# Attention units in four parts, their matmul order fixed over three units with dense work in shares

## The chip, the cores and the metric

The program runs on one NeuronCore of a Trainium2 chip; nothing is split over cores. The metric is device time in microseconds from the start of an execution to its end. The kernel before took 1500.14 us (median of three executions, 1498.36 to 1502.25). TensorE does the matmuls and the transposes, VectorE (DVE in the profile), ScalarE (ACT) and GpSimd (POOL) the elementwise work, SyncE (SP) issues the DMAs.

## What is computed

One layer of a diffusion backbone for two groups of tokens with the same weights: 512 latent tokens and 128 context tokens, model width 1024, all in float32. The kernel keeps both groups side by side as T = 640 tokens, five tiles of 128.

```
u = norm(x) * (1 + scale) + shift;  u = u @ w_in           # one wide projection feeds four mixers
A  HGRN2 linear recurrence                                  # stage "hgrn"
B  windowed attention (+-128 tokens) with a sink logit      # 8 query heads, 2 key heads, head width 64
C  latent attention: q = norm(cq) @ w_uq, k, v = c_kv @ w_ukv, plus a rotary part of 32   # 8 heads
D  grouped attention, q and k normalised, rotary            # 8 query heads, 2 key heads
   B, C, D: p = softmax(q k^T * scale); o = p v             # latent queries see 128 cached context keys + latent keys
y = (sum over the four of (o_n @ w_branch[n]) * sigmoid(gates_n)) @ w_out
x = x + gate1 * norm(y);  x = x + gate2 * norm(relu(norm(x).. @ w_mlp_in)^2 @ w_mlp_out)
```

The outputs are the new activations of both groups and the context group's keys, values and states.

## The kernel before

**Dense matmuls.** A float32 operand is split into a high part in the fp32r format and a rest, and each product is three matmuls: high x high, high x rest, rest x high (`t_steps`, lines 365 to 367, with tokens as the moving side in two halves of 320; `tok_block`, lines 381 to 383, with 128 tokens as weights). One step of `t_steps` for a gate is 8 x 3 = 24 matmuls of 320 columns. Gates (`gate_steps`) are 16 such steps per branch, `merge` multiplies a branch's output by its `w_branch` and adds it to `yT`.

**An attention unit.** `unit` (line 800) is one pair of heads for one tile of 128 queries. With five key tiles (W = 640, all latent queries of D and C) each head has its scores in an own PSUM tile `sc` (two buffers of two banks), then a maximum (DVE, line 818), the exponential with its sum (ACT, line 819), a reciprocal (DVE, line 821) and the division (POOL, line 809). With fewer key tiles (B, and the context queries) both heads share one `sc`. Then the ten (or fewer) probability tiles are transposed, four to a PSUM tile `tp` (line 856), and each `tp` is copied out to `PT`, the first and third by ACT (line 858), the second by DVE (line 860). `tp` has two buffers, which the output `pv` (line 1009 or 1185) shares. The output products are 64 columns wide for each head (`pv`, two per key tile, each two instructions in the trace), and `o_evac` splits the result (ACT line 506, DVE line 142).

**The three attention stages.** B (`run_gqa(1, ...)`, line 1017) and D (`run_gqa(3, ...)`, line 1029) have 20 units each, C (`mla`) has 4 head pairs of 5 units. In B and D the second half of the queries is made between the tenth and eleventh unit, and the gates come behind all units. In C each head pair `jj` first makes its own operands: two steps from `cq` into an `sc` bank, split by `q_split` (ACT line 777, DVE line 779); transposes of the rotary queries into `pj` (line 1152, copied out at 1157 and 1158); for even `jj` six steps for values into `pj` (copied out at 1166); two steps for keys into an `sc` bank, copied out by `k_evac` (ACT 795, DVE and POOL by line 142 and 139). `pj` and `ada_ps` are one buffer each in a PSUM pool `psx` that takes the place of the two `mm` banks during C. The 27 steps of the later modulation (`side`, line 211, a load of 512 KB for each) are given out three after each unit of C.

**What sets the order.** The program is recorded by a framework that puts the instructions of each engine in an order of its own: it runs a timeline of its own over the recorded work and gives an engine the next instruction that is ready there. So the order before is not that of the code: gates and merges stand between units. `in_order(PE)` (line 73) makes the matmuls recorded inside it keep their recorded order among themselves; before, only the hgrn stage used it. Matmuls recorded outside may still stand between them.

## Time and profile before

| what | value |
|---|---|
| median of three executions | 1500.14 us |
| the profiled execution | 1502.2 us |
| its span, first to last instruction | 1500.4 us |
| granted TensorE clock, mean | 0.991 |
| TensorE matmul busy | 1430.5 us (95%) |
| DVE, ACT, POOL busy | 796.1, 481.4, 432.2 us |
| stage B, between merges and next keys | about 333 to 481 us |
| stage D | about 560 to 690 us |
| stage C, operands of the first head pair | about 795 to 812 us |
| stage C, units | about 812 to 940 us |

How to read it: a matmul's busy time overlaps the next one's, so the time from one matmul's start to the next one's is what it costs TensorE; an idle time in brackets behind a row is what TensorE stood still before it, with the instruction whose end let it go. The stretches are read off the timeline: B's units with the work between them, D's, and C's.

### The profile page before, as it was taken

The numbers are of one execution on the slowest core, as the hardware profiler recorded it, in microseconds if no ns is written. First come the engines' busy times: TensorE is split into PE (matmuls) and PEld (weight loads), VectorE is DVE, ScalarE is ACT, GpSimd is POOL, SyncE is SP. The second block draws the span as 40 slices with busy tenths as digits, with TensorE's granted clock in tenths as the row PEclk, the third lists the DMA queues.
The fourth block names the chain that finished last, engine by engine and source line by source line (L and its number), as shares of the span: only waits on it lengthen the run. The fifth ranks groups of instructions, "written<-read, shape, count | busy, mean of one in ns | idle before, by whom it ended". The sixth has DMA issues, their size and how long they took to land.

```text
span 1500.4 us, 26709 instructions
## 1 busy us (share of the span) xinstructions
PE 1430.5 (95%) x10969; PEld 1302.2 (87%) x10969; DVE 796.1 (53%) x1447; ACT 481.4 (32%) x1161; POOL 432.2 (29%) x456
## 2 busy tenths in 40 slices
PE   6999999899999999999998998998999999999996
PEld 5898998899898998999996677988898998898995
DVE  4347657476643788433725566746243444444446
ACT  4334333333443235442124565225220110110112
POOL 2015325243321545222213334124111111112114
PEclk9999999999999999999999999999999999999998
DMA  9421212121112131112224601221343223222221
GB/s 328 128 85 58 70 49 64 50 68 50 45 43 59 34 84 37 33 42 74 80 68 143 224 15 43 99 85 56 112 129 101 80 71 98 71 70 71 75 66 70
DMA packets 138225, 121.17 MB, mean 81 GB/s; under 512 B 22296, under 2 KB 119412, under 8 KB 138104
## 3 DMA queue, kind: packets, MB, share of 16 engines
q1 hardware_dynamic: 138104, 119.47, 26.4%
q8 instruction: 86, 1.41, 0.4%
q14 instruction: 35, 0.29, 0.1%
HBM read 115.96 MB, written 3.49 MB: 80 GB/s over the span
## 4 chain that ended last, share of the span: by engine, by line
PE 70%; issue 13%; DVE 8%; POOL 5%; ACT 2%; DMA 1%; POOLq 0%; DVEq 0%; SPq 0%; ACTq 0%
PE mm L365 12%; PE mm L366 11%; PE mm L367 11%; PE mm L381 4%; PE mm L382 4%; PE mm L383 4%; PE tp L856 3%; POOL wh L139 3%; PE pv L1009 3%; PE sc L383 3%; PE sc L381 2%; PE sc L382 2%; PE sc L949 2%; PE sc L950 2%; DVE wl L142 1%
## 5 line engine op out<-in xcount | busy, mean ns | idle before, releaser
L139 POOL TENSOR_SCALAR wh<-wr 128x1024 fp32r<-128x1024 f32 (+3 forms) x136 | 156.7, 1154 | 536.4 <-PE mm L366 290.4
L142 DVE TENSOR_TENSOR wl<-wr,wh 128x1024 fp32r<-128x1024 f32 (+3 forms) x160 | 198.9, 1247 | 160.0 <-POOL wh L139 120.8
L365 PE MATMUL mm<-hTh,wh 128*128 128x320 f32 x704 | 220.5, 313 | 2.0 <-DVE qA L520 0.9
L367 PE MATMUL mm<-hTh,wl 128*128 128x320 f32 x704 | 219.2, 311 | 0.0
L366 PE MATMUL mm<-hTl,wh 128*128 128x320 f32 x704 | 218.2, 310 | 0.0
L366 PE MATMUL mm<-h2Tl,wh 128*128 128x320 f32 x512 | 159.4, 311 | 1.1 <-DVE h2Tl L142 1.1
L365 PE MATMUL mm<-h2Th,wh 128*128 128x320 f32 x512 | 159.5, 312 | 0.0
L367 PE MATMUL mm<-h2Th,wl 128*128 128x320 f32 x512 | 159.2, 311 | 0.0
L809 POOL TENSOR_SCALAR P<-P,rden 128x640 f32<-128x640 f32 (+3 forms) x120 | 84.5, 713 | 184.0 <-DVE rden L821 80.7
L365 PEld LDWEIGHTS mm<-hTh,wh 128*128 128x128 f32 x704 | 132.2, 188 | 3.9 <-DVE qA L520 1.0
L367 PEld LDWEIGHTS mm<-hTh,wl 128*128 128x128 f32 x704 | 132.2, 188 | 0.9 <-issue 0.7
L366 PEld LDWEIGHTS mm<-hTl,wh 128*128 128x128 f32 x704 | 132.2, 188 | 0.5 <-issue 0.3
L382 PE MATMUL mm<-wl,hidh 128*128 128x512 f32 x320 | 124.8, 390 | 0.6 <-DVE wl L142 0.6
L381 PE MATMUL mm<-wh,hidh 128*128 128x512 f32 x320 | 125.3, 392 | 0.0
L383 PE MATMUL mm<-wh,hidl 128*128 128x512 f32 x320 | 124.6, 389 | 0.0
L1292 ACT ACTIVATE relu<-mm 128x320 f32<-128x320 f32 x64 | 28.0, 438 | 281.1 <-PE mm L367 281.1
L366 PEld LDWEIGHTS mm<-h2Tl,wh 128*128 128x128 f32 x512 | 97.1, 190 | 1.7 <-DVE h2Tl L142 1.5
L365 PEld LDWEIGHTS mm<-h2Th,wh 128*128 128x128 f32 x512 | 96.9, 189 | 0.7 <-issue 0.4
L367 PEld LDWEIGHTS mm<-h2Th,wl 128*128 128x128 f32 x512 | 97.0, 189 | 0.0
L1293 DVE TENSOR_TENSOR relu<-relu 128x320 f32<-128x320 f32 x64 | 40.4, 632 | 100.8 <-ACT relu L1292 100.8
L1305 DVE TENSOR_TENSOR y<-mm,y 128x512 f32<-128x512 f32 x70 | 48.2, 689 | 81.9 <-PE mm L383 81.9
L381 PE MATMUL sc<-wh,hTh 128*128 128x256 f32 (+2 forms) x224 | 72.0, 322 | 5.5 <-DVE tx L935 2.4
(355 smaller groups left out, 3238.4 us busy)
## 6 DMA issues: line engine op xcount, KB each, us to landing
wr<-in_w_in SPq DMA_DIRECT2D x56, 512.0 KB, 3.7
wada<-in_w_ada SPq DMA_DIRECT2D x48, 512.0 KB, 4.5
wr<-in_w_mlp_in SPq DMA_DIRECT2D x32, 512.0 KB, 4.0
wr<-in_w_mlp_out SPq DMA_DIRECT2D x32, 512.0 KB, 3.6
wr<-in_w_in SPq DMA_DIRECT2D x64, 64.0 KB, 2.1
wr<-in_w_branch SPq DMA_DIRECT2D x8, 512.0 KB, 4.1
wr<-in_w_branch SPq DMA_DIRECT2D x16, 256.0 KB, 4.1
wr<-in_w_out SPq DMA_DIRECT2D x8, 512.0 KB, 3.6
```

The source lines that it names most:

```text
L139: G.tensor_scalar(out=out, in0=src, scalar1=1.0, scalar2=1.0, op0=ALU.mult, op1=ALU.mult)
L142: V.tensor_tensor(out=out, in0=src, in1=f(hi), op=ALU.subtract)
L365: PE.matmul(out=ps[:, 0:tn], lhsT=wh, rhs=a, start=(k == 0), stop=False)
L366: PE.matmul(out=ps[:, 0:tn], lhsT=wh, rhs=b, start=False, stop=False)
L367: PE.matmul(out=ps[:, 0:tn], lhsT=wl, rhs=a, start=False, stop=(k == nk - 1))
L381: PE.matmul(out=ps[:, 0:n], lhsT=a, rhs=w[k][0], start=(start and k == 0), stop=False)
L382: PE.matmul(out=ps[:, 0:n], lhsT=a, rhs=w[k][1], start=False, stop=False)
L383: PE.matmul(out=ps[:, 0:n], lhsT=b, rhs=w[k][0], start=False, stop=(stop and k == nk - 1))
L809: G.tensor_scalar(out=Pt[:, i, 0:W], in0=Pt[:, i, 0:W], scalar1=rden[:, i:i + 1], scalar2=1.0, op0=ALU.mult, op1=ALU.mult)
L856: PE.transpose(out=tp[:, kk, i], in_=Pt[:, i, 128 * (kt + kk):128 * (kt + kk) + 128], identity=ident)
L1009: PE.matmul(out=out, lhsT=Vt[:, ks[kt], 64 * a:64 * a + 64], rhs=PTa, start=start, stop=stop)
L1305: V.tensor_tensor(out=ys, in0=ps, in1=ys, op=ALU.add)
```

## The change

`unit` no longer emits a whole unit: it returns four parts, the scores of the first head (or of both, where they share a tile), the scores of the second, the transposes, and the output products. `run_units` emits them under `in_order(PE)` as a pipeline over three units: first scores of the new unit, products of the oldest, a share of dense work, second scores of the new unit, a share, transposes of the middle unit, a share. `Fill` gives out the dense work: in B and D the second queries (`query_steps`, 0.9 each) and the branch's 16 gate steps (1.0 each), 0.33 a share; in C the operands of the next head pair (`heads`, 0.25 a step and a share), now all through the one `pj` buffer, also the two `cq` steps and the two key steps that used `sc` banks. The first head pair's operands are made ahead of all units. The modulation steps are given out two after each unit's products, not three after each unit.

```diff
+    class Fill:
+        def __init__(self, steps):
+            self.steps, self.due = steps, 0.0
+        def give(self, share):
+            self.due += share
+            while self.due > 0:
+                self.due -= next(self.steps, 1e9)
+        def rest(self):
+            for _ in self.steps:
+                pass
...
-        if W > 512:
...
+        def wide(i):
+            sv = sc_tile()[:, :, 0:W // 2]
+            for a in range(2):
+                score(sv[:, a], i, a * (W // 2), W // 2)
+            V.tensor_reduce(out=negm[:, i:i + 1], in_=sv, axis=AX.XY, op=ALU.max, negate=True)
+            S.activation(out=Pt[:, i, 0:W].rearrange("p (a n) -> p a n", a=2), in_=sv, func=AF.Exp,
+                         bias=negm[:, i:i + 1], accum_out=den[:, i:i + 1])
+            V.reciprocal(out=rden[:, i:i + 1], in_=den[:, i:i + 1])
+            weigh(i)
+        def both():
...
         PT = at.tile([128, 5, 2, 128], F32, tag="PT", name="PT")
-        for j, kt in enumerate(range(0, nk, 2)):
-            kn = min(2, nk - kt)
-            tp = tp_tile().rearrange("p (k i) t -> p k i t", i=2)
-            for i in range(2):
-                for kk in range(kn):
-                    PE.transpose(out=tp[:, kk, i], in_=Pt[:, i, 128 * (kt + kk):128 * (kt + kk) + 128], identity=ident)
-            if j % 2 == 0:
-                S.activation(out=PT[:, kt:kt + kn], in_=tp[:, 0:kn], func=AF.Copy)
-            else:
-                V.tensor_copy(out=PT[:, kt:kt + kn], in_=tp[:, 0:kn])
-        o = pv_tile()
-        for kt in range(nk):
-            for a in range(2):
-                pv_mm(o[64 * a:64 * a + 64, 0:128], a, kt, PT[:, kt, a], kt == 0, kt == nk - 1)
-        o_evac(n, c, 128 * qt, o[:, 0:128])
+        def turn():
+            for j, kt in enumerate(range(0, nk, 2)):
+                kn = min(2, nk - kt)
+                tp = tp_tile().rearrange("p (k i) t -> p k i t", i=2)
+                for i in range(2):
+                    for kk in range(kn):
+                        PE.transpose(out=tp[:, kk, i], in_=Pt[:, i, 128 * (kt + kk):128 * (kt + kk) + 128], identity=ident)
+                if j % 2 == 0:
+                    S.activation(out=PT[:, kt:kt + kn], in_=tp[:, 0:kn], func=AF.Copy)
+                else:
+                    V.tensor_copy(out=PT[:, kt:kt + kn], in_=tp[:, 0:kn])
+        def products():
+            o = pv_tile()
+            for kt in range(nk):
+                for a in range(2):
+                    pv_mm(o[64 * a:64 * a + 64, 0:128], a, kt, PT[:, kt, a], kt == 0, kt == nk - 1)
+            o_evac(n, c, 128 * qt, o[:, 0:128])
+        if W > 512:
+            return lambda: wide(0), lambda: wide(1), turn, products
+        return both, lambda: None, turn, products
+    def run_units(units, beside, after=lambda: None):
+        cur = old = None
+        units = iter(units)
+        with in_order(PE):
+            while True:
+                new = next(units, None)
+                if new is None and cur is None and old is None:
+                    break
+                if new:
+                    new[0]()
+                if old:
+                    old[3]()
+                    after()
+                beside()
+                if new:
+                    new[1]()
+                beside()
+                if cur:
+                    cur[2]()
+                beside()
+                old, cur = cur, new
...
-        def queries(j2):
+        def query_steps(j2, Q):
             QQ = big(F32R, 2, 2, T, name="Q")
-            Q = [QQ[:, a] for a in range(2)]
+            Q += [QQ[:, a] for a in range(2)]
             wq = wgroup(q_cols(OFF[qn], j2), 0, 256)
...
                 q_split(tp[:, 0:2], [x[:, :, 128 * tt:128 * tt + 128] for x in Q], 0.125)
+                yield 0.9
+        def queries(j2):
+            Q = []
+            for _ in query_steps(j2, Q):
+                pass
             return Q
-        return queries, K, Vt
+        return queries, query_steps, K, Vt
...
-    def run_gqa(n, queries, Q0, K, Vt, tiles, sink, bands):
-        for j2 in range(2):
-            Q = queries(j2) if j2 else Q0
-            for qt, i in [(qt, i) for qt in range(5) for i in range(2)]:
-                ks, j = tiles(qt), 2 * j2 + i
...
+    def run_gqa(n, query_steps, Q0, K, Vt, tiles, sink, bands):
+        Q1, sig = [], [big(F32, 4, T, name="sig") for _ in range(2)]
+        second = query_steps(1, Q1)
+        def dense():
+            yield from second
+            yield from gate_steps(n, sig)
+        def units():
+            for j2 in range(2):
+                for qt, i in [(qt, i) for qt in range(5) for i in range(2)]:
+                    if j2:
+                        for _ in second:
+                            pass
+                    yield one(Q1 if j2 else Q0, j2, qt, i)
+        def one(Q, j2, qt, i):
+            ks, j = tiles(qt), 2 * j2 + i
...
+        fill = Fill(dense())
+        run_units(units(), lambda: fill.give(0.33))
+        fill.rest()
+        return sig
...
-    run_gqa(1, queries, Q0, K, Vt, swa_tiles, True, swa_bands)
-    sig = gates(1)
+    sig = run_gqa(1, query_steps, Q0, K, Vt, swa_tiles, True, swa_bands)
...
-        for jj in range(4):
+        def heads(jj, got):
             QQ = big(F32R, 4, T, name="mQ")
             Qa, QR = [QQ[:, a] for a in range(2)], [QQ[:, 2 + a] for a in range(2)]
             def ev(ps, t0, tn):
                 q_split(ps, [Qa[a][:, t0:t0 + tn] for a in range(2)], MS)
-            t_block(wu['uq'][0], 128 * jj, cX, ev, bank=sc_bank)
+            for _ in t_steps(wu['uq'][0], 128 * jj, cX, ev, bank=pj_tile):
+                yield 0.25
             for t4, tts in ((0, range(4)), (4, range(4, 5))):
                 tp = pj_tile().rearrange("p (i t) -> p i t", t=128)
                 n4 = len(tts)
                     V.scalar_tensor_tensor(out=to[32:64], in0=src, scalar=MS, in1=f(to[0:32]), op0=ALU.mult,
                                            op1=ALU.subtract)
                     copy_r(to[64:128], f(to[0:64]))
+                yield 0.25
             if jj % 2 == 0:
                 wv = [(x[0][:, 128 * jj:128 * jj + 256], x[1][:, 128 * jj:128 * jj + 256]) for x in wu['ukv'][1]]
                 for kt in range(6):
                     ps = tok_block(wv, 256, kX, kt, pj_tile())
                     for i in range(2):
                         S.activation(out=Vs[jj + i][:, kt], in_=ps[:, 128 * i:128 * i + 128], func=AF.Copy)
-            Vt = Vs[jj]
+                    yield 0.25
             K = new_K("mK")
             def ev(ps, t0, tn):
                 for a, b in ((t0, min(t0 + tn, T)), (max(t0, T), t0 + tn)):
                     if a < b:
                         k_evac(ps[:, a - t0:b - t0], K, a, b - a)
-            t_block(wu['ukv'][0], 128 * jj, kX, ev, halves=((0, 384), (384, 384)), bank=sc_bank)
-            for qt in range(5):
-                ks = full_tiles(qt)
-                def score(out, a, k0, kn):
-                    t = slice(128 * qt, 128 * qt + 128)
-                    b = slice(ks[0] * 128 + k0, ks[0] * 128 + k0 + kn)
-                    qk_mm(out, Qa[a][:, t], K_part(K, b.start, kn), a, last=False)
-                    PE.matmul(out=out, lhsT=QR[a][:, t], rhs=KRo[:, b], start=False, stop=True)
-                def pv_mm(out, a, kt, PTa, start, stop):
-                    PE.matmul(out=out, lhsT=Vt[:, ks[kt], 64 * a:64 * a + 64], rhs=PTa, start=start, stop=stop)
-                unit(n, jj, (0, 1), qt, len(ks), score, pv_mm)
-                side_steps(3)
+            for _ in t_steps(wu['ukv'][0], 128 * jj, kX, ev, halves=((0, 384), (384, 384)), bank=pj_tile):
+                yield 0.25
+            got += [Qa, QR, K]
+        got = [[] for _ in range(4)]
+        preludes = [heads(jj, got[jj]) for jj in range(4)]
+        for _ in preludes[0]:
+            pass
+        fill = Fill(iter(()))
+        def units():
+            for jj in range(4):
+                fill.rest()
+                fill.steps, fill.due = (preludes[jj + 1] if jj < 3 else iter(())), 0.0
+                for qt in range(5):
+                    yield one(jj, qt, *got[jj])
+        def one(jj, qt, Qa, QR, K):
+            ks, Vt = full_tiles(qt), Vs[jj]
...
+        run_units(units(), lambda: fill.give(0.25), lambda: side_steps(2))
```

The order on TensorE, at three places. In the names, `sc` is a PSUM tile of scores, `tp` of transposed probabilities `P`, `pv` of output products, `mm`, `mp` and `pj` of projections and small transposes; `hT`, `cq` and `ckv` are the normalised tokens and the latent query and key inputs, `w` weights, `ident` the identity of a transpose. Where a name has a number, each number is one use of a buffer.

TensorE in stage B before, around the products of one unit:

```order
L856 MATMUL tp<-ident,P 128x128 x4
L1009 MATMUL pv<-PT,Vt 64x128 x4
L382 MATMUL mm<-wl,hTh 128x256
L383 MATMUL mm<-wh,hTl 128x256
L919 MATMUL mp<-ident,txr 128x128 x2
L1009 MATMUL pv<-PT,Vt 64x128 x4
L856 MATMUL tp<-ident,P 128x128 x4
```

and in the changed kernel, in the same stage, around the products of one unit:

```order
L993 MATMUL sc<-K,Q 128x128
L994 MATMUL sc<-K,Q 128x128
L993 MATMUL sc<-K,Q 128x256
L994 MATMUL sc<-K,Q 128x256
L1067 MATMUL pv<-PT,Vt 64x128 x8
L365 MATMUL mm<-hTh,wh 128x320
L366 MATMUL mm<-hTl,wh 128x320
```

The products of a unit stood in two halves with other work between; now all of them stand in one piece, between the newest unit's scores and a share of dense work, and the eight transposes of the unit between stand together ahead of those scores. Counted over stage B, the runs of `pv` go from 35 to 20, in D from 21 to 20, in C from 25 to 21, and those of `ada_ps` in C from 18 to 13.

TensorE in stage D before, between two units:

```order
L856 MATMUL tp_6331<-ident_82,P_6299 128x128 x2
L919 MATMUL mp_6751<-ident_82,txr_6720 128x128 x2
L1009 MATMUL pv_6335<-PT_6318,Vt_5399 64x128 x10
L856 MATMUL tp_6371<-ident_82,P_6351 128x128 x4
L949 MATMUL sc_6456<-K_5397,Q_5663 128x320
L950 MATMUL sc_6456<-K_5397,Q_5663 128x320
```

and in the changed kernel:

```order
L367 MATMUL mm_6663<-hTh_138,wl_6660 128x320
L865 MATMUL tp_6689<-ident_82,P_6555 128x128 x4
L865 MATMUL tp_6695<-ident_82,P_6555 128x128 x4
L865 MATMUL tp_6701<-ident_82,P_6555 128x128 x2
L993 MATMUL sc_6710<-K_5397,Q_5663 128x320
L994 MATMUL sc_6710<-K_5397,Q_5663 128x320
```

Before, only the first of a unit's three `tp` tiles stood ahead of eight score matmuls and the other two behind them; now the three follow each other with nothing between, in each of the 16 units with five key tiles in D and the 16 in C.

TensorE at the start of stage C before:

```order
L365 MATMUL sc_9100<-ckv_7858,wh_8930 128x384
L366 MATMUL sc_9100<-ckv_7858,wh_8930 128x384
L367 MATMUL sc_9100<-ckv_7858,wl_8931 128x384
L1152 MATMUL pj_9033<-ident_82,qv_8938 64x128 x3
L211 MATMUL ada_ps_9008<-wada_9172,cpad_120 32x256 x4
L211 MATMUL ada_ps_9008<-wada_9178,cpad_120 32x256 x4
L211 MATMUL ada_ps_9008<-wada_9184,cpad_120 32x256 x4
L1152 MATMUL pj_9033<-ident_82,qv_8938 64x128
L949 MATMUL sc_9120<-mK_9088,mQ_9010 128x320
L950 MATMUL sc_9120<-mK_9088,mQ_9010 128x320
```

and in the changed kernel:

```order
L367 MATMUL pj_9022<-cq_7857,wl_8923 128x320
L1214 MATMUL pj_9033<-ident_82,qv_8938 64x128 x4
L1214 MATMUL pj_9044<-ident_82,qrp_8939 64x128
L381 MATMUL pj_9052<-wh_8930,ckv_7858 128x256
L382 MATMUL pj_9052<-wl_8931,ckv_7858 128x256
L383 MATMUL pj_9052<-wh_8930,ckv_7858 128x256
L381 MATMUL pj_9058<-wh_8930,ckv_7858 128x256
```

The operands of the first head pair used `sc` banks and `pj`, with modulation steps and scores between, and the values came behind the first scores; now twelve groups, two of `cq`, two of transposes, six of values, two of keys, follow each other in `pj`, and the first scores stand behind all of them.

## Rows read from the trace of the kernel before

**Rows 1.** The page, busy time and share of the span by engine:

```profile
PE 1430.5 (95%) x10969; PEld 1302.2 (87%) x10969; DVE 796.1 (53%) x1447; ACT 481.4 (32%) x1161; POOL 432.2 (29%) x456
```

**Rows 2.** Busy time by stretch: length, then PE, PEld, DVE, ACT, POOL, clock, DMA:

```profile
333.00:481.00 148.00, 147.14 (x1135) 133.74 (x1134) 80.14 (x191) 61.92 (x173) 42.72 (x58) 1.00 0.19 49
560.00:690.00 130.00, 127.06 (x1068) 119.00 (x1063) 65.47 (x141) 61.64 (x152) 42.09 (x52) 1.00 0.14 39
795.10:811.60 16.50, 12.47 (x94) 9.25 (x93) 11.72 (x26) 9.53 (x19) 9.38 (x14) 0.95 0.40 133
811.60:939.80 128.20, 116.74 (x1023) 90.72 (x1021) 77.54 (x168) 74.41 (x206) 50.12 (x75) 0.98 0.32 103
```

**Rows 3.** Waits of TensorE, in D and in C's units: total us, times, longest:

```profile
PE pv L1009 <- ACT PT L858: 1.6, 3, 0.7
...
PE pv L1185 <- ACT PT L858: 3.4, 5, 1.2
```

**Rows 4.** Timeline, TensorE in B: start, busy us, instruction, idle before:

```profile
390.96 0.44 PE L1009 MATMUL pv<-PT,Vt 128*64 128x128 f32 x4
391.32 0.66 PE L856 MATMUL tp<-ident,P 128*128 128x128 f32 x4
392.73 0.44 PE L856 MATMUL tp<-ident,P 128*128 128x128 f32 x2 [0.75 <-ACT PT L858]
...
449.23 0.31 PE L366 MATMUL mm<-hTl,wh 128*128 128x320 f32 x1
449.47 0.66 PE L1009 MATMUL pv<-PT,Vt 128*64 128x128 f32 x8
450.06 0.66 PE L856 MATMUL tp<-ident,P 128*128 128x128 f32 x4
```

**Rows 5.** Timeline, transposes of a unit of C and the copies behind them:

```profile
866.58 1.03 PE L856 MATMUL tp<-ident,P 128*128 128x128 f32 x8
867.21 0.60 ACT L858 ACTIVATE PT<-tp 128x512 f32<-128x512 f32 x1 [0.87 <-PE tp L856]
867.86 0.44 PE L856 MATMUL tp<-ident,P 128*128 128x128 f32 x2
```

**Rows 6.** Timeline of C: first matmul of a projection and its copy:

```profile
801.85 0.39 PE L365 MATMUL sc<-ckv,wh 128*128 128x384 f32 x1
802.62 0.98 ACT L795 ACTIVATE mK<-sc 64x384 fp32r<-64x384 f32 x2 [1.36 <-PE sc L367]
...
810.38 0.63 PE L1182 MATMUL sc<-ckv,mQ 128*128 128x320 f32 x1 [0.58 <-POOL mQ L139]
...
865.34 0.28 PE L381 MATMUL pj<-wh,ckv 128*128 128x256 f32 x1
865.90 0.28 ACT L1166 ACTIVATE mVt<-pj 128x128 f32<-128x128 f32 x1 [0.77 <-PE pj L383]
...
871.45 0.36 PE L365 MATMUL sc<-cq,wh 128*128 128x320 f32 x1
872.38 0.60 PE L1152 MATMUL pj<-ident,qv 128*64 128x128 f32 x4
872.58 0.88 ACT L777 ACTIVATE mQ<-sc 64x320 fp32r<-64x320 f32 x2 [0.89 <-PE sc L367]
```

**Rows 7.** Instructions of C by line and shape: count, busy us, mean ns, idle:

```profile
L819 ACT ACTIVATE P<-sc,negm 128x640 f32<-128x640 f32 x32 | 25.3, 794 | 14.9 <-DVE negm L818 13.0 <-DVE rden L821 1.4 <-POOL mQ L139 0.5
L819 ACT ACTIVATION_READ_ACCUMULATOR P<-sc,negm 128x1 f32 x32 | 6.4, 200 | 0.0
L1157 ACT ACTIVATE mQ<-pj 32x512 fp32r<-32x512 f32 x8 | 4.7, 585 | 3.1 <-DVE mQ L1158 2.3 <-PE pj L1152 0.6
...
L818 DVE TENSOR_REDUCE negm<-sc 128x1 f32<-128x640 f32 x32 | 26.4, 824 | 15.5 <-PE sc L1182 15.0
L779 DVE SCALAR_TENSOR_TENSOR mQ<-sc,mQ 64x320 fp32r<-64x320 f32 x16 | 7.8, 488 | 5.4 <-ACT mQ L777 5.2
L1158 DVE SCALAR_TENSOR_TENSOR mQ<-pj,mQ 32x512 fp32r<-32x512 f32 x8 | 5.5, 682 | 1.5 <-ACT mQ L1157 1.3
L142 DVE TENSOR_TENSOR mK<-sc,mK 64x384 fp32r<-64x384 f32 x8 | 4.4, 555 | 0.4 <-ACT mK L795 0.2
...
L809 POOL TENSOR_SCALAR P<-P,rden 128x640 f32<-128x640 f32 x32 | 25.5, 800 | 43.1 <-DVE rden L821 36.1 <-PE pj L383 6.8
L139 POOL TENSOR_SCALAR mK<-mK 64x768 fp32r<-64x768 f32 x8 | 7.5, 934 | 7.6 <-DVE mK L142 7.2
```

67 lines of the change are left out of this document (29 added, 38 removed).

## The prediction

> **What bounds the kernel now.** The page first: TensorE is busy 1430.5 us of the 1500.4 us span, no other engine above 53% [rows 1]. So the time is TensorE's matmuls plus what it stands still, and no matmul is added or taken away by the change: only its order moves, and with it the idle time and the small costs of going from one kind of matmul to another. How much there is to win stands in the view by stretches [rows 2]. In B TensorE is busy 147.14 of 148.00 us, so 0.86 is idle; in D 127.06 of 130.00, idle 2.94; where C makes its first head pair's operands 12.47 of 16.50, idle 4.03; in C's units 116.74 of 128.20, idle 11.46. All four together are 19.3 us, 1.3% of the time. The list of waits says what the largest single items are: the output products wait for ACT's copies of the transposed probabilities, 1.6 us in D and 3.4 in C's units [rows 3]. The timelines then give the price of a step [rows 4 to 6], the groups by line the durations of the other engines' parts [rows 7].
>
> The sum is made against the profiled execution, 1502.2 us (span 1500.4 and 1.8 around it), which is 2.1 above the median of 1500.14.
>
> **Stage B.** The rows before have products in two runs of four, 390.96 to 391.32, so 0.36 us a run, and in one run of eight, 449.47 to 450.06, so 0.59 [rows 4]. Two runs of four cost 2 x 0.36 - 0.59 = 0.13 more. A run also costs its entry: the dense matmul ahead of it takes 449.23 to 449.47, 0.24, where six dense matmuls in a row take 871.45 to 872.38, 0.155 each [rows 6], so 0.09. Together 0.22 for a run that goes, and B loses 15 of its 35: -3.3. Of the 0.86 idle I take 0.7 away, because a whole step of dense work now stands between a unit's transposes and its products, which covers the 0.75 wait for a copy that the rows show once [rows 4]. B: -4.0; bounds -4.2 and 0 (if a run's entry depends on its neighbours and not on its being one more).
>
> Gates that come behind all units in the code now come among them; in the order before they already stood among units, so nothing is gained by that again. VectorE, ACT and POOL have the same work.
>
> **Stage D.** The same argument takes away the 2.94 idle; one product run less is nothing. But the three `tp` tiles of a unit with five key tiles now follow each other, `tp` has two buffers, and the third tile needs the first one's copy. The one place in the rows that has this order shows the price: transposes start at 866.58, ACT's copy starts at 867.21 and takes 0.60, the third tile's transposes start at 867.86, so 1.28 behind the first [rows 5]. Eight transposes by themselves take some 0.8 to 0.9 (the eight are busy 1.03, the two 0.44, so 0.1 for each further one). The wait is 0.4 to 0.5; I take 0.42. What is queued behind it on TensorE is the next unit's scores and the oldest unit's products, so nothing fills it. 16 units: +6.7. D: -2.9 + 6.7 = +3.8. Bounds for a unit: 0, if the split order before lost as much in changes of kind, and 0.75, the longest wait for such a copy in these rows.
>
> **Start of C.** Twelve groups through the one buffer `pj`, with nothing between: each must be copied out before the next one's first matmul. The chain by rows:
> two halves of the queries, each 1.13 from first matmul to ACT's copy (871.45 to 872.58), 0.44 for one of its two ACT instructions and two VectorE instructions of 0.488 [rows 6, 7]: 2 x 2.55 = 5.1;
> four rotary transposes 0.60, ACT 0.585, VectorE two of 0.682 [rows 6, 7]: 2.6, and the fifth by itself 1.2 (my estimate, a quarter of the columns, the fixed part stays);
> six value groups, 0.56 to the copy (865.34 to 865.90) and two copies of 0.28 [rows 6]: 6.7;
> the first key half 0.77 (801.85 to 802.62), 0.49 for ACT, two VectorE instructions of 0.555 [rows 6, 7]: 2.4; the second half until its last part has gone through VectorE and POOL (0.934, [rows 7]) and is multiplied: 3.0.
> Together 21.0 us. It begins where the key projection stood, less the twelve query matmuls that were done earlier: 801.85 - 12 x 0.155 = 800.0. First scores are then complete at 821.0. Before, their last part starts at 810.38 [rows 6] and they are complete at about 811.3. The step costs +9.7. The values' 18 matmuls are then done (a credit of some 2.2) and the modulation steps that filled the stretch before are not (a debit of about the same). C's start: +10. Bounds: +7 (the queue of copies split better between ACT and VectorE) and +12.
>
> The Trainium skill, "Perfetto Trace Analysis", section "Matmuls", speaks against this step: independent matmul groups should rotate through different PSUM banks, so that the copying out of one overlaps the next one's matmuls. The trace agrees so far as it goes: where the key halves used `sc` banks, ACT's copy of one ran beside the other's matmuls. By the rule alone, the loss would be the copies' part of the chain above, some 14 of the 21, and the sum 4 higher.
>
> **Units of C.** What goes: the 11.5 idle, all of it, because dense groups stand between a unit's parts; four product runs (25 to 21) and five modulation runs (18 to 13) by 0.22 each: -2.0. What comes: twelve units more with the three `tp` tiles in a row (four had it already), 12 x 0.42 = +5.0. And the next head pairs' groups go through the one `pj` as well, one a share. For the second head pair I walk through it, from the start of the first scores, with the durations above, each queue in order and ACT's exponential (0.794 and 0.200, [rows 7]) ahead of the copy that follows it, as the changed program has it:
> scores 0 to 0.9, VectorE's maximum (0.824) to 1.85, exponential to 2.95; the first query group is multiplied 0.9 to 1.9, but ACT's copy of it starts at 2.95 and VectorE is done at 4.4. The second scores end at 2.8, and the second query group waits for `pj` from there: 1.6. Its copy waits in the same way for the second exponential and VectorE is done at 7.8; it was multiplied by 5.4, so the rotary group waits 2.4. The fifth transpose waits 2.0 behind VectorE, where the next unit's maximum stands between the two halves of the rotary copy; the first key group 1.2; and a `tp` tile 1.2, because ACT has the key copy ahead of it.
> Together 8.4. The third and fourth head pairs have a unit's products and modulation steps between some of the groups; the same walk gives about 7 and 6. (The value groups' open part of 0.6 is covered.) That is 21. The lower bound is without exponentials in the way: only what a copy takes longer than the scores or transposes (0.9, 1.28) that stand between two shares: 3.7 in the second head pair, 1.2 in each of the others, 6 in all. I take 18, near the walk, since its order is that of the queues, with a little off because single steps may be shorter in a row. While TensorE waits there, the middle unit's transposes and the newest unit's scores are queued behind. Sum for the units: -11.5 - 2.0 + 5.0 + 18 = +9.5.
>
> Other queues: the 27 loads of 512 KB for the modulation go out two a unit instead of three, and the DMA share in this stretch is 0.32 [rows 2], so they come in time. On POOL the keys' copies (0.934) can stand ahead of a division (0.800); the transposes of that unit come a unit later (scores 0.9 twice, transposes 1.28, products and modulation steps some 1.8: 4.9 at least), and a head's chain of maximum, exponential and division is 0.82 + 0.99 + 0.80 = 2.6, so I cost it at nothing; without the cover it is 0.9 for each of six.
>
> **Sum.** -4.0 + 3.8 + 10 + 9.5 = +19.3. 1502.2 + 19.3 = 1521.5 for an execution like the profiled one, 1519 for the median.
>
> **Rivals.**
> *The clock falls* (slower still). The start of C had a granted clock of 0.95 with TensorE busy 12.47 of 16.50 us, where B and D had 1.00 with next to no idle [rows 2]. In the new chain TensorE has some 6.6 us of matmuls in 21. If the clock goes to the 1.2 GHz level there, each of them takes twice as long, and they are all in the chain: +6.6, and some 2.4 in the first unit behind it, +9 in all: 1528. Against it: 0.95 is still near full.
> A sentence apart: the Trainium skill, "TensorE: Matmul & The Clock Gate", Part 1, has the clock follow TensorE's activity, which is what would make this rival happen.
> *Covered after all* (no change). The projections' waits in C's units vanish, because the scheduler's order on ACT and VectorE puts the copies ahead and scores, products and modulation steps cover them: -4.0 + 3.8 + 10 - 11.5 - 2.0 + 5.0 = +1.3: 1503.5, less 2.1, so 1501.
> *All covered* (faster). The third tile also costs no more than the split order did: -4.0 - 2.9 + 10 - 11.5 - 2.0 = -10.4, so 1490. It rests on one mechanism, whether ACT's copy of the first `tp` tile is out by the time the eighth transpose is done; it decides against me if ACT's copies start less than 0.25 behind a tile's first transpose. For it: each part now lies a whole part behind what it needs, and the softmax chain of 2.6 is shorter than a unit. Against it: [rows 5] shows the copy's start at 0.63. That the order isn't what the change says is no rival here: the rows of the order show it.
>
> **How the numbers follow.** Forecast 0.62, by itself 1504 to 1530 (C's start 7 to 12, the waits in C's units 6 to 21, D's tiles 0 to 12, B -4.2 to 0). Clock 0.16, no change 0.11, faster 0.11. The range 1499 to 1533 holds the forecast, the clock and the case without change, and leaves the faster one out. A measurement of this kernel tells about 0.3% from no change, so from 1495.6 to 1504.6: faster 0.11, same 0.11, slower 0.78.
>
> **What would show it.** In the changed profile: B's stretch shorter by 3 to 4 us with hardly an idle row; in D about 16 waits of `tp` for ACT's copy, 0.4 each; ahead of C's first scores about 20 us in which TensorE is busy a third, with `pj` waiting for VectorE and ACT; in C's units `pj` waits of some 18 us, and products that no longer wait for ACT. The prediction is wrong if the first scores of C stand within 5 us of where they stood, or if `pj` hardly waits inside the units, or if the time is won in D and B beyond 7 us, which no row here would explain.

## The result: 5% slower, where 1.3% was forecast

The changed kernel takes 1574.41 us (median of four, 1572.3 to 1580.63) against 1500.08 (median of four; the 1500.14 above is that of three): a ratio of 1.0502, 95% interval 1.0469 to 1.0534. Forecast were 1519 and a range to 1533. The direction was right, the size was not: 74 us where 19 stood in the sum. (Of y3_gates_behind below, one execution, the profiled one, ran at a mean clock of 0.2 and took 6678 us; it stands in no time here.)

The page of the changed kernel, its busy time and its clock line (40 slices of the span; 9 is nine tenths or more), and under it the clock line of the kernel before:

```profile
PE 1447.7 (92%) x10969; PEld 1318.1 (84%) x10969; DVE 795.6 (51%) x1447; ACT 483.8 (31%) x1161; POOL 432.3 (28%) x456
...
PEclk9999999999999999999996799999999999999999
...
PEclk9999999999999999999999999999999999999998
```

Against [rows 1] the matmuls are the same 10969, VectorE, ACT and POOL work as long as before, and TensorE is busy 17 us longer for the same work. That fits the clock: in the stages below 51 us of its busy time fall at the 1.2 GHz level and not 10, and half of the difference, some 21 us, would be the loss if matmuls take twice as long there (an estimate from these numbers). The other 53 us of the 70 that the span grew are TensorE standing still.

Where they went is read by cutting both traces at equal points: the same matmul, with the same matmuls done by then (the first scores of B, the first scores of D, the first matmul on `cq`, 73 matmuls later, the end of C's units). Lengths in us, from the timelines:

| kernel | median us | ratio, interval | B | D | C, first operands | C, units |
|---|---|---|---|---|---|---|
| before | 1500.1 | | 200.8 | 268.2 | 10.7 | 136.2 |
| changed | 1574.4 | 1.0502 (1.0469 to 1.0534) | 206.3 | 296.0 | 34.0 | 150.6 |

Behind these points both kernels need 558 us, the same to a few tenths. (The prediction's own C start ended with complete scores, 3 to 5 us later, so C is best read as one: 146.9 against 184.6.)

Busy time by stretch: length, then PE, PEld, DVE, ACT, POOL, clock, DMA, for B, D and C's two parts, in the kernel before and then in the changed one:

```profile
326.10:526.90 200.80, 195.25 (x1488) 180.38 (x1487) 117.33 (x290) 75.92 (x207) 64.96 (x85) 0.99 0.21 51
526.90:795.10 268.20, 264.64 (x2006) 255.05 (x2006) 140.47 (x298) 89.67 (x234) 80.17 (x96) 1.00 0.22 60
795.10:806.40 11.30, 9.50 (x78) 7.36 (x76) 9.31 (x21) 7.82 (x15) 5.34 (x7) 1.00 0.16 49
806.40:942.10 135.70, 122.01 (x1056) 94.71 (x1055) 80.74 (x177) 76.87 (x212) 54.17 (x82) 0.97 0.34 109
...
325.10:531.40 206.30, 193.19 (x1489) 181.99 (x1488) 114.20 (x288) 74.24 (x207) 67.58 (x86) 0.98 0.21 49
531.40:827.40 296.00, 274.81 (x2007) 260.92 (x2006) 143.43 (x300) 92.77 (x234) 77.78 (x96) 0.98 0.21 54
827.40:860.80 33.40, 16.23 (x72) 12.31 (x72) 11.87 (x24) 11.57 (x29) 8.14 (x12) 0.68 0.05 16
860.80:1011.90 151.10, 124.36 (x1059) 98.48 (x1060) 78.46 (x173) 73.90 (x198) 51.91 (x77) 0.90 0.30 98
```

What the reader is to see: D stood idle for 3.6 us and C's first operands for 1.8, and now it is 21 and 17; and the granted clock of C's first operands is 0.68, a mean of the 1.2 and the 2.4 GHz level. The busiest of the other engines, VectorE, is busy for 36% to 55% of these stretches. So no other engine is full, and yet TensorE waits.

For whom it waits in the first 70 us of D: total us, times, longest:

```profile
PE mp L957 <- DVE rden L826: 5.5, 1, 5.5
PE mm L365 <- DVE sig L1024: 3.5, 1, 3.5
PE mp L957 <- DVE ms L196: 2.0, 1, 2.0
PE tp L865 <- ACT PT L867: 1.6, 2, 0.9
PE mm L381 <- DVE tx L979: 1.3, 1, 1.3
PE mp L957 <- DVE txr L775: 1.1, 1, 1.1
```

The output products' wait of [rows 3] isn't in this list, as the change wanted (behind 600 us, D still has one of 1.9). What stands there now is `mp` (the transposes of a second query step) and the merge, and both wait for VectorE. The longest one, in the timeline of that place (TensorE, VectorE and POOL; start, busy us, instruction, idle before):

```profile
585.85 2.06 POOL L139 TENSOR_SCALAR wh<-wr 128x1024 fp32r<-128x1024 f32 x2
...
586.40 0.39 ACT L974 ACTIVATE tx<-mm 128x256 f32<-128x256 f32 x1 [2.40 <-PE mm L383]
...
586.93 2.05 DVE L142 TENSOR_TENSOR wl<-wr,wh 128x1024 fp32r<-128x1024 f32 x1 [1.95 <-POOL wh L139]
...
588.88 0.31 PE L994 MATMUL sc<-K,Q 128*128 128x320 f32 x1
588.90 0.40 DVE L976 TENSOR_REDUCE ssq<-tx 128x4 f32<-128x256 f32 x1
...
592.10 0.16 DVE L196 TENSOR_SCALAR ms<-ssq 128x4 f32<-128x4 f32 x1
...
593.40 0.42 DVE L979 TENSOR_TENSOR tx<-mm,rs 128x256 f32<-128x256 f32 x1
593.86 0.70 DVE L981 TENSOR_TENSOR tx<-tx,qg_b 128x256 f32<-128x256 f32 x1
594.48 0.15 DVE L826 RECIPROCAL rden<-den 128x1 f32<-128x1 f32 x1
594.71 0.66 PE L957 MATMUL mp<-ident,tx 128*128 128x128 f32 x2 [5.51 <-DVE rden L826]
```

Read it from below. The transposes at 594.71 need the normalised queries, a chain of ACT, VectorE, POOL and VectorE again behind the projection that ended at 586.4. VectorE could have begun at 586.8, but next in its queue is the split of a gate's weights (`wl`). It had been waiting 1.95 us for POOL's half, starts at 586.93 and takes 2.05; so the sum of squares starts at 588.90. A maximum, a split of queries and another weight split, rows that are left out here, stand in the chain's way after that: its next link (`ms`) starts only at 592.10. TensorE has its next scores, transposes and gates behind these two small transposes and may do none of them. (The list names `rden`, the last VectorE instruction that ended before; what was needed is `tx` ahead of it.) Before, the framework was free to put other work there.

In C's units the list is that of the one buffer:

```profile
PE pj L1214 <- DVE mQ L784: 6.9, 3, 2.4
PE tp L865 <- ACT PT L867: 4.2, 11, 0.8
PE pj L365 <- DVE mQ L784: 3.3, 3, 1.2
PE pj L365 <- DVE mQ L1220: 2.6, 2, 1.3
PE mm L365 <- DVE rden L826: 1.8, 1, 1.8
PE pj L1214 <- DVE mQ L1220: 1.7, 1, 1.7
PE pj L381 <- DVE mQ L1220: 1.3, 1, 1.3
```

The `pj` rows shown are 15.8 us, 17.0 with one shorter row.

### The profile page after: what moved, and what is told of

Same layout as the page of the kernel before. It is cut to its first block, busy times and chain, and to the rows that moved or that the text cites. A ratio compares the mean times of both kernels' runs of the same rounds, so it can differ in the third digit from the quotient of the medians.

```text
span 1570.5 us, 26738 instructions
## 1 busy us (share of the span) xinstructions
PE 1447.7 (92%) x10969; PEld 1318.1 (84%) x10969; DVE 795.6 (51%) x1447; ACT 483.8 (31%) x1161; POOL 432.3 (28%) x456
## 4 chain that ended last, share of the span: by engine, by line
PE 65%; issue 13%; DVE 9%; ACT 5%; POOL 5%; DMA 1%; SPq 0%; POOLq 0%; DVEq 0%; ACTq 0%
PE mm L365 11%; PE mm L366 11%; PE mm L367 11%; PE mm L381 4%; PE mm L382 3%; PE mm L383 3%; POOL wh L139 3%; PE sc L383 2%; PE sc L381 2%; PE sc L382 2%; PE tp L865 2%; PE pv L1067 2%; PE sc L993 2%; PE sc L994 1%; DVE wl L142 1%
## 5 line engine op out<-in xcount | busy, mean ns | idle before, releaser
L865 PE MATMUL tp<-ident,P 128*128 128x128 f32 x456 | 71.4, 286 | 14.7 <-ACT PT L867 11.6
```

The lines of the kernel that those rows point to most:

```text
L865: PE.transpose(out=tp[:, kk, i], in_=Pt[:, i, 128 * (kt + kk):128 * (kt + kk) + 128], identity=ident)
```

## The experiments

Fifteen kernels, told in nearly the order in which they ran. The stage columns are cut at the points above. A ratio is against executions of the kernel before that were taken together with that kernel; their medians lie between 1501.4 and 1502.7, so differences of medians across the table are good to some 2 us.

| run | median us | ratio to before, interval | B | D | C, first | C, units |
|---|---|---|---|---|---|---|
| x1_free | 1533.2 | 1.0216 (1.0190 to 1.0242) | 208.5 | 280.6 | 13.4 | 144.8 |
| x2_c_before | 1534.6 | 1.0219 (1.0196 to 1.0241) | 204.5 | 295.1 | 10.7 | 134.6 |
| x3_late | 1560.9 | 1.0402 (1.0375 to 1.0429) | 206.0 | 285.9 | 34.0 | 148.5 |
| x4_sc_banks | 1548.8 | 1.0316 (1.0301 to 1.0331) | 205.0 | 297.8 | 18.4 | 141.0 |
| y1_third | 1561.7 | 1.0402 (1.0385 to 1.0418) | 206.3 | 290.5 | 35.2 | 145.8 |
| y2_side_first | 1568.1 | 1.0441 (1.0417 to 1.0464) | 204.6 | 295.2 | 13.6 | 166.8 |
| y3_gates_behind | 1582.0 | 1.0529 (1.0510 to 1.0549) | | | | |
| y4_dummy | 1565.4 | 1.0426 (1.0407 to 1.0444) | 204.8 | 294.3 | 31.4 | 146.3 |
| z1_three | 1530.8 | 1.0204 (1.0171 to 1.0237) | 206.0 | 283.1 | 18.7 | 136.2 |
| z2_free_sc_gates | 1510.9 | 1.0059 (1.0035 to 1.0084) | 206.9 | 275.7 | 10.7 | 130.3 |
| z3_free_sc | 1517.0 | 1.0104 (1.0077 to 1.0131) | 206.7 | 282.0 | 10.7 | 131.2 |
| z4_three_side | 1536.2 | 1.0227 (1.0197 to 1.0257) | 208.8 | 283.1 | 10.8 | 145.8 |
| w1_queries_between | 1496.4 | 0.9965 (0.9953 to 0.9977) | 200.8 | 269.8 | 10.7 | 129.7 |
| w3_share_half | 1498.3 | 0.9977 (0.9967 to 0.9987) | 202.3 | 269.8 | 10.7 | 129.9 |
| w4_side_three | 1496.8 | 0.9965 (0.9952 to 0.9977) | 200.8 | 269.8 | 10.7 | 131.9 |

**x1_free: is it the fixed order?**

```diff
-        with in_order(PE):
+        if True:
             while True:
```

> The changed kernel with the four parts, shares and pipeline as they are, but TensorE's order inside the attention stages left to the framework again. Three theories for the 74 us. (Order) TensorE's fixed order makes it stand still for copies that are queued in order on VectorE and ACT; then the loss goes with the fixed order: 1500, give or take 8. (Parts) the loss is in the way the units are cut and the dense work is dealt out, whoever orders it: over 1550. (Clock) the loss starts with TensorE's granted clock, 68 us of the changed profile at the 1.2 GHz level against 10 before; it goes only as far as the thin stretches go, so it can't be told from (Order) here, but would show half-speed stretches left over.

1533.2: some 41 of the 74 us go with the fixed order, the other 33 stay. So neither theory holds alone. C as one comes down from 184.6 to 158.2. The 13.4 of its first part is by equal counts: modulation steps stand between the groups again, while C's first scores still come 37.3 us behind the first matmul on `cq` (33.4 in the changed kernel). D gives back 15, B nothing.

**x2_c_before: C by itself.** Stage C's part of the change taken back (its old loop over head pairs, the four parts of a unit called one behind the other).

```diff
+        for jj in range(4):
...
+            for qt in range(5):
...
+                for part in unit(n, jj, (0, 1), qt, len(ks), score, pv_mm):
+                    part()
+                side_steps(3)
...
-        run_units(units(), lambda: fill.give(0.25), lambda: side_steps(2))
```

> The changed kernel with stage C as before (units whole, operands of a head pair through the score banks, three modulation steps a unit, no fixed order); B and D as changed. (Order): each stage loses by itself; between equal points of the two traces C lost 22 us ahead of its first scores and 15.5 in its units, so 37.6 come back: 1537. (Rival) the waits of D and C are coupled, by the clock or by work that D leaves over for C: under 1525, or over 1548.

1534.6: 40 us come back, where the equal points said 37.6. B and D keep 204.5 and 295.1, so the stages lose separately and their losses add.

**x3_late: the query transposes.**

```diff
             if tt + 1 < NT:
                 ps = tok_block(wq, 256, hT, tt + 1, bank())
+            yield 0.9
             tp = (mp_tile if j2 else tp_tile)()
...
-            yield 0.9
```

> The changed kernel with one line moved: the two transposes of a query step are given out one share later than the projection of the next one, not directly behind it. (Order): in D the transposes waited for the chain of the query normalisation, 2.0 + 1.1 + 5.5 us in the list of waits, and the projections behind it 1.3 more; these 10 us go, and 3 or so of half clock with them: 1561. (Rival) the wait is VectorE's queue as a whole (weight splits stand in it), and the next matmul takes it over: 1570 or more.

1560.9, as expected: D 10.1 shorter, with its `mp` waits 2.1 us in one place:

```profile
PE mp L958 <- DVE rden L826: 2.1, 1, 2.1
PE mm L381 <- DVE tx L979: 1.8, 2, 1.2
PE tp L865 <- DVE ol L142: 1.6, 1, 1.6
PE tp L865 <- ACT PT L867: 1.4, 4, 0.7
PE mm L365 <- DVE sig L1024: 1.0, 2, 0.6
```

The merge's wait for `sig`, 3.5 us in the list of D above, is 1.0 in this run, though the merge wasn't edited: a wait for VectorE can change by an edit elsewhere.

**x4_sc_banks: the one buffer.**

```diff
-            for _ in t_steps(wu['uq'][0], 128 * jj, cX, ev, bank=pj_tile):
+            for _ in t_steps(wu['uq'][0], 128 * jj, cX, ev, bank=sc_bank):
...
-            for _ in t_steps(wu['ukv'][0], 128 * jj, kX, ev, halves=((0, 384), (384, 384)), bank=pj_tile):
+            for _ in t_steps(wu['ukv'][0], 128 * jj, kX, ev, halves=((0, 384), (384, 384)), bank=sc_bank):
```

> The changed kernel with the query and key groups of C's head pairs in the two score buffers again (as before the change) and not in the one pj buffer; all else as changed. (Order, single buffer): ahead of C's first scores a query half no longer waits for the other's copies (2.1 + 2.1 + 2.3 us in the list of waits, and the clock): 8 less there; in the units the waits of pj for the query and key copies, some 11 us, go: 1556. (Rival) the score buffers are held by the units' own scores, so the groups wait for exponentials instead: 1570 or more.

1548.8: 25.7 us come back, 7 more than expected; 15.6 instead of 8 in C's first part, where scores now stand ahead of and among the value groups (the first score at 841.2, the first value group at 847.1), and 9.6 in the units. No other single edit that keeps the fixed order gives back as much.

**y1_third: the third tile of transposes.**

```diff
                 if old:
-                    old[3]()
-                    after()
+                    old[4]()
                 beside()
+                if old:
+                    old[3]()
+                    after()
```

> The changed kernel with the third tile of a unit's transposes moved: it stands behind the next unit's first scores and a share of dense work ahead of that unit's products, instead of directly behind the second tile. (Third tile): 32 units pay some 0.43 each for the copy of the first tile, 13.8 in all, of which the additional runs give back 0.1 each: 1564. (Rival) the products wait for the third tile's copy instead, or the scores' buffers: 1571 or more.

In this diff the fifth part is the third tile. 1561.7, 12.7 us less: 5.5 in D and 4.8 in C's units; C's first operands are 1.2 longer, and behind C, where nothing was edited, the run is 2.2 shorter. The price is the one that [rows 5] gave. Third tile of a unit of D in the changed kernel, TensorE:

```profile
604.93 1.03 PE L865 MATMUL tp<-ident,P 128*128 128x128 f32 x8
606.28 0.44 PE L865 MATMUL tp<-ident,P 128*128 128x128 f32 x2 [0.31 <-ACT PT L867]
606.47 0.39 PE L993 MATMUL sc<-K,Q 128*128 128x320 f32 x1
```

From 604.93 to 606.28 it is 1.35, where [rows 5] had 1.28. The idle time in brackets, 0.31, is less than what is lost, since a matmul's modelled end lies behind the next one's start.

**y2_side_first: useful work in the thin chain.**

```diff
         for _ in preludes[0]:
-            pass
+            side_steps(1)
```

> The changed kernel with one modulation step recorded behind each group of the first head pair's operands, so that TensorE has useful work in the chain ahead of C's first scores (34.0 us there now, 22 of them at the 1.2 GHz level). (Clock follows the thin chain): it stays up, the chain shrinks to about 27, and the units have 12 steps of 0.42 less: 1560. (Clock independent, or loads not there in time): the stretch stays at 32 or more and only the 5 us of moved steps come back: 1569.

1568.1: the stretch by equal counts shrinks to 13.6, but only because other matmuls are counted in it; C as a whole goes from 184.6 to 180.4. The steps have their own wait there (3.6 us in four places for `wada` loads), and the clock is low for 47.8 us in C instead of 51.2. Mostly the second theory.

**y4_dummy: the clock by itself.**

```diff
-        for _ in preludes[0]:
-            pass
+        with in_order(PE):
+            for g, _ in enumerate(preludes[0]):
+                idle = tp_tile()
+                for k in range(5 if 4 <= g < 10 else 14):
+                    PE.transpose(out=idle[:, k % 4], in_=qr[k % 4][:, 0:128], identity=ident)
```

> The changed kernel with 142 needless transposes (14 behind each query, rotary and key group of the first head pair, 5 behind each value group, 0.1 us each at full clock) whose results nobody reads; nothing else is changed, so any gain is the granted clock's. (Clock): the stretch ahead of C's first scores goes from 34 us to 27 or so, and the first units lose their half-speed part, 5 more: 1562. (Rival: the low clock is only a sign of the waits and costs little) the work is added and the time is 1575 or more.

(They are 114 transposes, not 142: six groups of 14 and six of 5.) 1565.4: some 11 us of needless work (at 0.1 each) make the kernel 9 us faster; the two intervals don't overlap. The same stretch, with the dummies:

```profile
824.50:855.90 31.40, 24.92 (x189) 22.12 (x188) 12.71 (x26) 12.32 (x31) 8.52 (x13) 1.00 0.06 18
```

The clock stays at 1.00 (0.68 before in it), and the chain is shorter by 2 to 3 us. C's units behind it give 4.3 more (20.5 us at the 1.2 GHz level there instead of 29.2). B and D, which the edit doesn't touch, are 3.2 shorter in this run, with 13.6 instead of 20.5 us at the low level; that part isn't the edit's. Without the added transposes TensorE's order in C is that of the changed kernel, row for row. So the clock's share ahead of C's scores and right behind them is some 7 us, near the 9 of the rival, and the chain is thin for its own reasons: 31.4 at full clock.

**y3_gates_behind: gates outside the order.** The gate steps recorded behind all units and outside the fixed order; the second queries stay in the shares.

```diff
             yield from second
-            yield from gate_steps(n, sig)
...
         fill.rest()
+        for _ in gate_steps(n, sig):
+            pass
         return sig
```

> The changed kernel with the gate steps of B and D recorded behind all units and outside the fixed order, as before the change; units and second queries keep the fixed order. (Deal): TensorE stands still in B and D because a fixed share is all it has at a wait; with the gates free to go into any gap, 12 to 20 us come back: 1558. (Order): the waits of the query steps and third tiles belong to the ordered matmuls themselves and a gate can stand there only if the framework's own timeline shows the gap: 1570 or more.

1582.0, no faster than the changed kernel (the intervals overlap): the number of the second theory, but not its reason. The columns of stages are left out; TensorE's order can be read from its trace. The gates do stand between the ordered matmuls of D, often 17 between a unit's transposes, but they are used up early: the last units of D have none left. What that costs wasn't measured.

**z1_three: do the single gains add up?** The diffs of x3_late, x4_sc_banks and y1_third together.

> The changed kernel with three edits together, each run alone before: query transposes one share later (13.5 us by itself), third tile later (12.7), query and key groups of C in the score buffers (25.7). The fixed order and the shares stay. (Separate waits): the three stand at different places and add up, 51.9: 1522. (One queue): VectorE and ACT are what the order waits for, so a wait taken away turns up at the next ordered matmul: 1535 or more.

1530.8: 43.6 of 51.9. In the stages they nearly add up: C's units 136.2, just 150.6 less 4.8 less 9.6; D 283.1, where 280.4 would be the sum. So the theory of separate waits is mostly right, and yet the fixed order is still 30 us behind the kernel before, 15 of them in D and 8 ahead of C's scores.

**z2, z3: how the work is recorded, with TensorE's order free.** Both leave the order to the framework and use the score buffers; z3 keeps the gates in the shares, z2 records them behind the units. The diffs are those of x1_free and x4_sc_banks, and for z2 that of y3_gates_behind.

> The four parts and the three-unit pipeline as the changed kernel records them, but TensorE's order left to the framework, C's query and key groups in the score buffers, and the gate steps recorded behind all units. (Deal): of the 33 us that were left without the fixed order, some 20 in B and D come from recording the gates among the units (as they are then no longer held back to fill gaps) and 11 in C from the one buffer; without both the time is that of the kernel before: 1502. (Parts) the cut of the units itself costs: 1512 or more.

> The same with the gate steps among the units, as the changed kernel deals them; TensorE's order left to the framework, C's groups in the score buffers. (Deal): 20 us above the run with the gates behind: 1522. (Parts): the two agree within 5.

1510.9 and 1517.0: 6 us for the gates among the units, not 20, and B and D still 13.6 over the kernel before in z2 (19.7 in z3). But C was 5 to 6 shorter than before in both.

**w1_queries_between: the last part.** z2 with the second queries of B and D recorded between the tenth and eleventh unit again, and their units recorded whole, one behind the other.

```diff
         def units():
             for j2 in range(2):
+                Q = list(query_steps_all(query_steps, j2)) if j2 else Q0
                 for qt, i in [(qt, i) for qt in range(5) for i in range(2)]:
...
-        fill = Fill(dense())
-        run_units(units(), lambda: fill.give(0.33))
-        fill.rest()
-        return sig
+        for parts in units():
+            for part in parts:
+                part()
+        return gates(n)
```

> The run with free order, score buffers and gates behind, with the second queries of B and D recorded between the tenth and eleventh unit again, so B and D are recorded as before and only C has the pipeline of parts and its operands dealt in shares. (Dealt queries): B and D go back to 201 and 268 us between equal points, C keeps its gain of 6: 1495, faster than before. (Cut of the units): B and D stay some 10 us longer: 1508. (C's gain was chance of the clock): B and D as before, C too: 1501.

1496.4, 0.35% faster than before (interval 0.23 to 0.47). TensorE's order in B and D is now that of the kernel before, row for row, and so are their lengths to 1.6 us. Two things were taken back here together, the dealt queries and the pipeline of parts in B and D; which of them cost z2 its 14 us wasn't separated. What remains is C's gain, in stretches of B, D, C's first operands and C's units:

```profile
327.30:528.20 200.90, 195.37 (x1489) 180.46 (x1488) 117.38 (x290) 75.92 (x207) 64.95 (x85) 0.99 0.21 51
528.20:797.90 269.70, 266.14 (x2005) 256.40 (x2005) 140.41 (x298) 89.67 (x234) 80.13 (x96) 0.99 0.22 60
797.90:809.00 11.10, 9.31 (x78) 7.32 (x76) 9.09 (x21) 7.81 (x15) 5.11 (x7) 1.00 0.16 48
809.00:938.30 129.30, 118.50 (x1059) 93.02 (x1056) 79.15 (x177) 75.65 (x212) 54.73 (x83) 1.00 0.34 115
```

In the units TensorE is idle 10.8 us (13.7 before at the same points) and the clock is 1.00 (0.97 before); before, 6.8 us ran at the lower level there. How much of the 6.5 us is idle time and how much the clock wasn't separated. The gain itself isn't one trace's chance: z2 and z3 have w1's order in C, row for row, and took 141.0 and 141.9 for all of C, w1 140.4; x2_c_before has the order of the kernel before there, and they took 145.3 and 146.9.

**w3_share_half and w4_side_three** vary w1: operands dealt at twice the pace, and three modulation steps a unit.

```diff
-        run_units(units(), lambda: fill.give(0.25), lambda: side_steps(2))
+        run_units(units(), lambda: fill.give(0.5), lambda: side_steps(2))
...
-        run_units(units(), lambda: fill.give(0.25), lambda: side_steps(2))
+        run_units(units(), lambda: fill.give(0.25), lambda: side_steps(3))
```

> The same with the operands of C's next head pair dealt at twice the pace (two groups a share). (Earlier operands help): they are ready sooner and the units' scores wait less, 2 us under the run before it. (No difference): the framework sets TensorE's order anyway, the same within 2 us. (Crowding): more copies stand together on ACT and VectorE: 3 us over it.

> The same as the first with three modulation steps after each unit's products as before the change. (Loads): TensorE waits more for the modulation weights, as 3 of C's waits in the runs show: 2 us over. (Fill): the earlier steps fill waits of the first units: 2 us under. Else the same.

1498.3 and 1496.8: no difference that the intervals tell, for both.

**z4_three_side** adds the diff of y2_side_first to z1.

> The three edits together and one modulation step behind each group of the first head pair. (Clock follows the thin chain): the chain ahead of C's first scores is already short with the score buffers (18.4 us, 7 of them at half clock), so only 3 to 5 us come back against the three edits alone: 1518. (Loads): the steps wait for their weights there, as 3.6 us of waits showed, and nothing comes back: 1522 or more.

1536.2, no faster than without (the intervals overlap): C's first operands go from 18.7 to 10.8 by equal counts and C's units from 136.2 to 145.8. Nothing came back, which is what the theory of loads said; that the loads are the reason wasn't shown (TensorE waits 2.9 us for them in C, and 6.4 in one place for the rotary copies).

**The ladder.** Five kernels lead from the fastest to the changed one: second queries dealt among the units and units in parts in B and D, +14.4 (w1 to z2); gates among them, +6.2 (z3); C's groups through the one buffer, +16.2 (x1); TensorE's order fixed, +41.2 (changed). Together 78.0, from 1496.4 to 1574.4. The last step costs 26.4 in C and 15.4 in D and gives back 2.2 in B.

## Why the prediction was wrong

**What bounds the kernel.** Right: TensorE's idle time and its order. But the step "What goes: the 11.5 idle, all of it, because dense groups stand between a unit's parts", taken for D too ("the same argument takes away the 2.94 idle"), took the view of one kernel's idle time as the most that order can do. The 19 us were what was left after the framework had put something ready at each place; the order that replaces it can lose far more.

**Stage B, -4.0: failed.** It is 5.5 longer. The pieces are there, the products in one piece, but the dense work that was to cover them has waits of its own: the merge's `yT` (1.9 us), four waits of 0.7 to 1.3 us in the first units, for POOL's division and for copies, and one of 1.5 later. The price of a run is borne out in its direction, but was too high: B's products cost 16.4 us without idle time where 18.4 stood, so 2.0, not 3.3.

**Stage D, +3.8: failed, and worst: +27.8.** The third tile was sized rightly: 5.5 us came back in D and 4.8 in C when it was moved, [rows 5] was the price. The step that failed is the 2.94 of idle time that dense work was to take away: second queries and gates were counted as filler that costs nothing, and D's idle time between equal points went from 3.6 to 21.2. A query step is a projection and two transposes with a chain over three engines between, and the transposes stood right behind the next projection; that cost 10.1 in D (x3_late). What makes up the other 12 isn't shown. Along the ladder D goes from 269.8 to 275.7, 282.0, 280.6 and 296.0, so 6.3 came with the dealt gates and 15.4 with the fixed order. The timeline above shows weight splits of dealt gates in VectorE's queue, in front of what TensorE waits for, and the merge of B's output, which lay between D's first three units before, now stands whole behind the first scores; no run took either back alone. "VectorE, ACT and POOL have the same work" was true (795.6 us against 796.1 in [rows 1]) and didn't settle the question: the chain above shows that their order counts too. A smaller omission: I counted the runs of products that go, but not that a unit's scores now stand in two runs instead of one; in D the 144 score matmuls cost 25.3 us without idle time in x3_late, which had only 3.4 us at the low clock there, and 22.2 before.

**Start of C, +10, and units, +9.5: half of it.** Together 37.7. The mechanism was the right one, and x4_sc_banks bears it out; the sizes failed. The start, to complete scores as in the sum, lost 20.5 (from 16.2 to 36.7 behind the first matmul on `cq`). In the units the walk over the second head pair gave 8.4 and for all pairs 21, taken 18; the list shows 17.0. Ahead of the first scores the chain was to be 21.0; from the first group at 834.74 to complete scores at 864.1 it was 29.4, at full clock (y4_dummy) 25.5. Two links were read wrongly. VectorE starts on a query half only behind both of ACT's instructions, so a half takes 3.2 to 3.3 and not 2.55; and the rotary copies of two heads go through ACT and VectorE one behind the other, not side by side:

```profile
835.98 0.88 ACT L782 ACTIVATE mQ<-pj 64x320 fp32r<-64x320 f32 x2 [1.29 <-PE pj L367]
836.88 0.99 DVE L784 SCALAR_TENSOR_TENSOR mQ<-pj,mQ 64x320 fp32r<-64x320 f32 x2 [0.99 <-ACT mQ L782]
...
841.22 1.03 PE L1214 MATMUL pj<-ident,qv 128*64 128x128 f32 x4 [2.08 <-DVE mQ L784]
842.28 0.59 ACT L1219 ACTIVATE mQ<-pj 32x512 fp32r<-32x512 f32 x1 [2.24 <-PE pj L1214]
842.90 0.68 DVE L1220 SCALAR_TENSOR_TENSOR mQ<-pj,mQ 32x512 fp32r<-32x512 f32 x1 [1.83 <-ACT mQ L1219]
843.62 0.59 ACT L1219 ACTIVATE mQ<-pj 32x512 fp32r<-32x512 f32 x1 [0.75 <-DVE mQ L1220]
844.24 0.68 DVE L1220 SCALAR_TENSOR_TENSOR mQ<-pj,mQ 32x512 fp32r<-32x512 f32 x1 [0.66 <-ACT mQ L1219]
845.07 0.39 PE L1214 MATMUL pj<-ident,qrp 128*64 128x128 f32 x1 [2.82 <-DVE mQ L1220]
```

The rotary link took 3.85 where 2.6 stood (3.42 in y4_dummy, at full clock). The token projections ahead of the chain were a second miss: they take 7.4 us, with two waits of 1.7 and 1.5 for their copies, where the sum began 4.9 behind the first matmul on `cq`, because the query groups that stood between them before are now behind them. The credit for the 11.5 us of idle time in the units, all of it, was too much: 26.7 are idle there, 17 for `pj`, and ten that have other reasons, four of them the third tile.

The rule cited there, the Trainium skill, "Perfetto Trace Analysis", section "Matmuls" (independent groups rotate through different banks), would have made the sum 4 us higher than mine; two buffers for a part of the groups gave back 25.7 (x4_sc_banks), so the case agrees with the rule, and by more than those 4.

**The clock, a rival at 1528.** It did fall: the attention stages ran 72 us at the 1.2 GHz level against 10 before. y4_dummy puts its share in C at some 7 us; the 9 of the rival were well sized and its base was wrong. What the clock cost in B and D, with 20.5 us at the low level against 3.4 before, no run separated.

**The rivals on the other side.** "All covered" was wrong as a whole, but its half for C lives in w1: the pipeline of parts and the dealt operands there are together worth some 5 us, if nothing fixes TensorE's order and the query and key groups have the score buffers.

## What to carry to other kernels

Fixing an engine's order is only as good as the orders of the engines that feed it: for every matmul in the fixed row write down the chain behind it and what stands ahead of each link in VectorE's, ACT's and POOL's queues, the weight splits too. Dense work is filler only if it needs nothing that is produced nearby; a projection that is followed by its own normalisation and transposes is a chain, and its second half belongs later (x3_late moved it by one share and gained 13.5 us). When a long order is replaced, size the loss by what the old order had hidden, not by the idle time it had left, and try the new recording without the fixed order first.

## What the runs showed of the hardware

Needless matmuls can pay: 114 transposes put into a stretch where TensorE was busy 16.23 of 33.40 us kept the granted clock at 1.00 instead of 0.68, and the kernel was 9 us faster, some 7 of it in that stage.
